# Layer two's output product by seven products for half of two column blocks, the spatial masks delayed, and the last block's copies rearranged

## The chip, the cores and the metric

The kernel runs on one core of a Trainium2 chip. The metric is device time in microseconds (us), the median of three runs. TensorE multiplies, VectorE (DVE) and ScalarE (ACT) do elementwise work, GpSimd (POOL) a little of it, and SyncE (SP) starts most of the transfers. Each engine executes its own instructions in the order in which the program issues them, and waits where an instruction's input or its buffer isn't ready.

## The reference

Two layers over 256 tokens of width 2048, all in fp32:

```python
def reference(x, ...):
    for l in range(DEPTH):                                   # 2
        h = rms_norm(x, norm1_g[l])
        z = h @ w_in[l]                                      # [sgu u | sgu v | q | k | v]
        z_sgu = jax.nn.gelu(z[..., :2 * SGU_WIDTH], approximate=False)
        out_a = chunked_sgu(z_sgu, sgu_norm_g[l], sgu_w[l], sgu_b[l])
        out_b = swa_sink_attention(...)                      # 16 heads, 4 groups, window 128
        mixed = jnp.concatenate([rms_norm(out_a, out_norm_a[l]),
                                 rms_norm(out_b, out_norm_b[l])], axis=-1)
        x = x + mixed @ w_out[l]                             # 2048 x 2048
        h2 = rms_norm(x, norm2_g[l])
        x = x + (jax.nn.silu(h2 @ w_gate[l]) * (h2 @ w_up[l])) @ w_down[l]
    return x

def chunked_sgu(z, v_norm_g, w_s, b_s):
    u, v = jnp.split(z, 2, axis=-1)
    v = rms_norm(v.reshape(...), v_norm_g)                   # 16 heads, chunks of 128
    w = w_s * jnp.tril(jnp.ones((CHUNK, CHUNK), w_s.dtype))
    gate = jnp.einsum('hts,bcshd->bcthd', w, v) + b_s.T[None, None, :, :, None]
    return u * gate.reshape(b, s, SGU_WIDTH)
```

The feed-forward width is 5632.

## The kernel before

**The unit of work.** TensorE takes an fp32 product as three products of rounded operands (type fp32r): `mm3` (lines 149 to 151) multiplies high part by high, high part by the weight's low part, and low part by the weight's high part. A weight tile of 256 x 512 is loaded by `raw_load` on SP (line 106, 512 KB, eight buffers). `split2` casts it to its high part `wh` on ACT (line 115, five buffers) and forms the low part `wl` on DVE (line 116, four buffers). A `unit` multiplies one such tile with both token halves: 2 x 2 x 3 = 12 matmuls of 128x512 into two PSUM banks.

**Order.** The program is issued in one stream, and each engine keeps that order. A unit advances a clock by one (`tick`), a half unit by 0.5; side work (norms, transposes, attention) is put into the stream by `later(delay, fn)` when the clock gets there. PSUM has eight banks: five for products (`acc`), two beside (`dacc`), one small (`sm`). Small products (transposes, attention, spatial gate) take their bank in turn from `sm`, `dacc`, `dacc`, `acc`.

**Normalising.** `inv_rms` writes mean square plus epsilon `ms` on DVE (line 203) and takes its power of -1/2 on POOL (`ir`, line 205). POOL's queue also holds the bias loads (line 516) and, per half of the spatial gate, the load of `wm` (line 607) with the triangular mask directly behind it (`affine_select`, line 608). Line 639 scales `v` by `ir` on DVE.

**The output product.** `mixed @ w_out` has four column blocks of 512 (0 to 3) and two halves: `a` (spatial gate, four pairs of 128 rows) and `b` (attention, likewise). A part such as a1 is half `a` of column block 1: four units, each of one pair, into two banks. When a part is whole, DVE adds it to the residual `xres`, scaled by that half's inverse rms (line 757, one instruction per token half). When both parts of a block are whole, `norm_block` takes the block's transposes for the second norm. The table `PARTS` sets the order in which the units of the parts are issued, one row per layer. The pairs are made from transposes (`ps_t`, line 222) by `split_gain`: ACT writes the high part with the gain (line 212), DVE the low part (line 213), into `aT`.

**Seven products.** Feed-forward blocks and part of the q projection use `seven`, a scheme with seven products of half-size operands instead of eight (2 x 2 blocks of the token halves against the even and odd tiles of k, by two column blocks). It needs sums of the operands: sums of weight tiles (on DVE, line 332, or by transfers that add, on POOL) and sums of activation tiles, formed by `combine`: `g` on ACT (line 266), `e` in three DVE instructions (lines 274 and 277 are the first two), the split into `ext` on ACT and DVE (line 287). Its products lie in five banks.

**The end.** The last product, `w_down`, adds into banks that were seeded with the residual. `out_of` copies a finished bank to SBUF on ACT (line 889) and stores it from SP (line 891); in the last column block each token half goes in two quarters.

Of the kernel before, what the change touches and what calls it, by code (L numbers as in the profile page):

```python
# [12 lines left out]
F32 = mybir.dt.float32  # L13
# [7 lines left out]
P = 128  # L21
# [42 lines left out]
END_AT = (((22, 26), (30, 32)), ((22, 27), (31, 33)))  # L64
FF_FIRST = 5
EXT_AT = (6.5, 8, 11, 13, 16, 18, 21.5, 24)
GATE_LOAD = ((24, 29), (5, 15))
PARTS = (
    "a0 a0 a1 a1 a0 a0 a1 a1 a2 a2 a2 a2 a3 a3 a3 a3 b0 b0 b1 b1 b0 b0 b1 b1 b2 b2 b2 b2 b3 b3 b3 b3",
    "a0 a0 a1 a1 a0 a0 a1 a1 b0 b0 b0 b0 b1 b1 b1 b1 a2 a2 a2 a2 b2 b2 b2 b2 a3 a3 a3 a3 b3 b3 b3 b3",  # L70
# [14 lines left out]
def trunk(ctx, tc, x, xt, w_in, w_q, w_out, w_gate, w_up, w_down, sgu_w, sgu_g, consts,  # L85
# [206 lines left out]
    def combine(ps, lay, col, ext):  # L292
# [4 lines left out]
        extend(g, ap, "big", ext)  # L297
        return pair

    def seven(src, pairs, ext, out, end=lambda sg: None, soon=False, by_dma=(), put_off=False):  # L300
# [79 lines left out]
        yield  # L380

# [41 lines left out]
    for lay in range(L):  # L423
# [180 lines left out]
        def gate_load(b, lay=lay, wms=wms):  # L604
            wm = ap.tile([P, 8, P], F32, tag="big", name="wm", bufs=8)
            with tc.issue_after(anchor[0].ins):
                nc.gpsimd.dma_start(wm, sgu_w[lay, :, 8 * b : 8 * b + 8, :])
            nc.gpsimd.affine_select(
                out=wm, in_=wm, pattern=[[0, 8], [1, P]], compare_op=ALU.is_ge, fill=0.0,
                base=0, channel_multiplier=-1,  # L610
            )
            wms[b] = wm

# [39 lines left out]
        pairs_a = []  # L653

        def u_gated(b, acc, lay=lay, layer=layer, gate=gate, ssa=ssa, pairs_a=pairs_a):
# [79 lines left out]
        def finish_mixed(kind, ss, rstds=rstds):  # L735
            rstds[kind] = finish_rms(ss, SW)

# [140 lines left out]
        def down(blocks, lay=lay, pairs_f=pairs_f, norm_block=norm_block, ss1=ss1, pairs1=pairs1, ext1=ext1, left=left, live=live, release=release, accs=accs, full=full, seed=seed, flush=flush, turn_over=turn_over):  # L878
# [4 lines left out]
            def out_of(n, t, acc):  # L883
                parts = 2 if last and n == ND - 1 else 1
                w = NB // parts
                for i in range(parts):
                    cs = slice(n * NB + i * w, n * NB + (i + 1) * w)
                    xs = xres[:, t, cs]
                    nc.scalar.copy(xs, acc[:, i * w : (i + 1) * w])
# [160 lines left out]
```

## Time and profile before

| what | us |
|---|---|
| three runs | 1920.44 to 1922.36, median 1920.5 |
| the profiled execution | 1919.74 |
| its span | 1918.0 |
| TensorE busy, 0 to 200 us | 195.81 |
| TensorE busy, 1000 to 1146.6 us | 146.58 |
| TensorE busy, 1146.6 to 1212 us | 65.40 |
| TensorE busy, 1212 to 1400 us | 188.00 |
| TensorE busy, 1800 to 1918 us | 113.50 |
| DVE busy in the same five stretches | 159.66, 105.88, 46.25, 172.99, 82.76 |

The span is the time from the first to the last event of the profiled execution. The granted TensorE clock is 1.00 throughout, and the core moves 453.71 MB at a mean of 237 GB/s. In a group of the profile, `x` is followed by the count, then by busy time and mean ns of one, and then by the idle time of the engine just before these instructions and the releaser that ended most of it. In a timeline, a row is start, duration, engine, line, operation, output<-inputs, and in brackets the wait before it and what ended it. In a table by window, the columns are the sum, then the busy time of PE, PEld, DVE, ACT and POOL (count in parentheses), then granted clock, DMA share and GB/s.

### The profile page before, as it was taken

The page shows a single profiled execution, that of the slowest core. Times are in us where ns is not written, and L with a number is a line of the kernel's source. Part 1 is how long each engine was busy: PE and PEld are TensorE (multiplying, and loading weights), DVE is VectorE, ACT ScalarE, POOL GpSimd, SP SyncE. Part 2 cuts the span into 40 slices and gives each one's busy share as a digit, 9 for nine tenths or more (in the row PEclk, how much of TensorE's full clock was granted, in tenths as well). Part 3 has the DMA queues.
Part 4 walks back from the last instruction along what each step waited for, and adds up shares of the span by engine and source line. Part 5 has one row for each costly group of instructions (what it writes and reads, how often), then busy time and mean ns, then how long its engine had stood idle before and what let it go on. Part 6 is the DMA issues. An engine that isn't in the chain of part 4 may idle for free.

```text
span 1918.0 us, 25387 instructions
## 1 busy us (share of the span) xinstructions
PE 1909.3 (100%) x8788; PEld 1571.2 (82%) x8788; DVE 1693.5 (88%) x1826; ACT 1343.2 (70%) x1799; POOL 170.0 (9%) x172
## 2 busy tenths in 40 slices
PE   9999999999999999999999999999999999999999
PEld 7878888888888888888888888888888888888887
DVE  7986689999999999999796767799999999999993
ACT  8668576677667676777777576566877677766774
POOL 0221001000100001000011200000000100010000
PEclk9999999999999999999999999999999999999999
DMA  9874348788877897888577534587789778888783
GB/s 354 260 272 159 136 160 238 257 243 283 262 238 248 270 290 228 247 256 287 187 220 258 188 126 164 179 265 234 246 264 295 231 248 260 282 239 254 252 274 110
DMA packets 126707, 453.71 MB, mean 237 GB/s; under 512 B 14065, under 2 KB 14705, under 8 KB 126577
## 3 DMA queue, kind: packets, MB, share of 16 engines
q1 hardware_dynamic: 105264, 375.52, 53.0%
q0 software_dynamic: 20736, 75.51, 21.2%
q8 instruction: 69, 1.13, 0.2%
q10 hardware_dynamic: 576, 1.05, 0.2%
q14 instruction: 62, 0.50, 0.1%
HBM read 449.92 MB, written 2.10 MB: 236 GB/s over the span
## 4 chain that ended last, share of the span: by engine, by line
PE 94%; issue 1%; DVE 1%; DMA 1%; POOL 1%; ACT 0%; SPq 0%; ACTq 0%; DVEq 0%; POOLq 0%
PE m L150 14%; PE m L149 14%; PE m L151 14%; PE dacc L149 10%; PE dacc L150 10%; PE dacc L151 10%; PE acc L149 6%; PE acc L151 5%; PE acc L150 5%; PE ps_f L222 1%; PE ps_v L578 1%; DMA wm<-in_sgu_w_dram 1%; DVE wl L116 1%; PE ps_s L529 1%; POOL ir L205 1%
## 5 line engine op out<-in xcount | busy, mean ns | idle before, releaser
L115 ACT CAST wh<-raw 128x1024 fp32r<-128x1024 f32 (+1 forms) x794 | 815.9, 1050 | 417.6 <-DVE raw L332 166.9
L116 DVE TENSOR_TENSOR wl<-raw,wh 128x1024 fp32r<-128x1024 f32 (+1 forms) x794 | 945.3, 1219 | 106.0 <-PE acc L150 29.3
L149 PE MATMUL m<-wh,ext 128*128 128x512 f32 x704 | 276.7, 393 | 0.0
L150 PE MATMUL m<-wl,ext 128*128 128x512 f32 x704 | 274.9, 390 | 0.0
L151 PE MATMUL m<-wh,ext 128*128 128x512 f32 x704 | 274.4, 390 | 0.0
L150 PE MATMUL dacc<-wl,aT 128*128 128x512 f32 x624 | 243.3, 390 | 0.0
L149 PE MATMUL dacc<-wh,aT 128*128 128x512 f32 x624 | 243.2, 391 | 0.0
L151 PE MATMUL dacc<-wh,aT 128*128 128x512 f32 x624 | 243.0, 389 | 0.0
L116 DVE TENSOR_TENSOR wl<-t,wh 128x1024 fp32r<-128x1024 f32 x176 | 213.3, 1222 | 12.7 <-issue 5.2
L115 ACT CAST wh<-t 128x1024 fp32r<-128x1024 f32 x176 | 184.4, 1051 | 38.0 <-DVE t L333 14.1
L150 PE MATMUL m<-wl,hT 128*128 128x512 f32 x528 | 205.8, 390 | 1.7 <-DVE wl L116 1.7
L149 PE MATMUL m<-wh,hT 128*128 128x512 f32 x528 | 206.4, 391 | 0.0
L151 PE MATMUL m<-wh,hT 128*128 128x512 f32 x528 | 205.6, 389 | 0.0
L150 PEld LDWEIGHTS m<-wl,ext 128*128 128x128 f32 x704 | 132.2, 188 | 28.7 <-DVE wl L116 1.8
L149 PEld LDWEIGHTS m<-wh,ext 128*128 128x128 f32 x704 | 132.2, 188 | 27.6 <-ACT wh L115 0.9
L151 PEld LDWEIGHTS m<-wh,ext 128*128 128x128 f32 x704 | 132.1, 188 | 27.5
L149 PEld LDWEIGHTS dacc<-wh,aT 128*128 128x128 f32 x624 | 117.1, 188 | 25.2 <-ACT wh L115 0.8
L150 PEld LDWEIGHTS dacc<-wl,aT 128*128 128x128 f32 x624 | 117.2, 188 | 24.7 <-DVE wl L116 0.6
L151 PEld LDWEIGHTS dacc<-wh,aT 128*128 128x128 f32 x624 | 117.1, 188 | 24.4
L149 PE MATMUL acc<-wh,aT 128*128 128x512 f32 x336 | 135.0, 402 | 0.0
L151 PE MATMUL acc<-wh,aT 128*128 128x512 f32 x336 | 131.5, 391 | 0.0
L150 PE MATMUL acc<-wl,aT 128*128 128x512 f32 x336 | 130.9, 390 | 0.0
(151 smaller groups left out, 2717.0 us busy)
## 6 DMA issues: line engine op xcount, KB each, us to landing
raw<-in_w_gate_dram SPq DMA_DIRECT2D x176, 512.0 KB, 5.8
raw<-in_w_up_dram SPq DMA_DIRECT2D x176, 512.0 KB, 5.7
raw<-in_w_down_dram SPq DMA_DIRECT2D x176, 512.0 KB, 5.7
t<-in_w_gate_dram POOLq DMA_DIRECT2D x80, 512.0 KB, 7.4
raw<-in_w_in_dram SPq DMA_DIRECT2D x76, 512.0 KB, 5.7
raw<-in_w_out_dram SPq DMA_DIRECT2D x64, 512.0 KB, 3.2
raw<-in_w_up_dram POOLq DMA_DIRECT2D x40, 512.0 KB, 6.0
raw<-in_w_q_dram SPq DMA_DIRECT2D x32, 512.0 KB, 5.2
```

What stands on the lines that cost most here:

```text
L115: nc.scalar.copy(wh[:, j : j + step, :], src)
L116: nc.vector.tensor_tensor(wl[:, j : j + step, :], src, f(wh[:, j : j + step, :]), ALU.subtract)
L149: nc.tensor.matmul(acc, ah, wh, start=first, stop=False, skip_group_check=again)
L150: nc.tensor.matmul(acc, ah, wl, start=False, stop=False, skip_group_check=again)
L151: nc.tensor.matmul(acc, al, wh, start=False, stop=last, skip_group_check=again)
L205: anchor[0] = nc.gpsimd.tensor_tensor(r, ms, mhalf[:, :n], ALU.pow)
L222: nc.tensor.transpose(ps[:, j, t * P : (t + 1) * P], blocks[t][:, j * P : (j + 1) * P], ident)
L529: nc.tensor.matmul(ps[r][:, i, :], qT[gp][rows, i0 + i, t * P : (t + 1) * P], kT[rows, gp, :nk], start=True, stop=True,)
L578: nc.tensor.matmul(pv[:, r, i], pt[:, (r * n + i) * (t + 1) + b, :], zkv[b][:, cols], start=b == 0, stop=b == t,)
```

## The change

Three edits go together.

**Layer two's output product.** Half `a` of column blocks 2 and 3, which was two parts of four units, becomes fourteen steps "s" of `seven_low`: seven products of two halves each, a half being six matmuls. It uses three banks, `l0`, `l1` and `l2`, in place of `seven`'s five. The weights come from a new host array `w_oa`, the same values in another order. Per two pairs, the tiles x and b22 take raw buffers, `ys` and `ss` take buffers of the tag "hT"; DVE adds two sums (lines 433 and 434), POOL issues two adding transfers (lines 435 and 440). ACT copies bank l0 into l1 once and two partial results into `mp`; DVE adds to these, and adds the four results to the residual (`residual`, at one step each, two with the negated inverse rms `na`). The pairs of half `a` are now made by `combine_a`, which also makes the sums `ext`. While steps "s" are open, small products take their bank from three places and not four. The table's second row sets where the steps stand among the units of a0, a1, b0 and b1.

**Masks.** The triangular mask is issued 5 (layer two: 4) clock units after its load and behind the last power or transfer that POOL has been given by then.

**Last copies.** In the last column block only the second token half goes in two quarters; the second quarter is copied by DVE, and the first quarter's store is issued by ACT's queue.

```diff
--- before.py
+++ after.py
+S_OUT = (False, True)
+EXT_A_WAIT = 0.5
+MASK_AFTER = ((5, 5), (4, 4))
...
-    "a0 a0 a1 a1 a0 a0 a1 a1 b0 b0 b0 b0 b1 b1 b1 b1 a2 a2 a2 a2 b2 b2 b2 b2 a3 a3 a3 a3 b3 b3 b3 b3",
+    "a0 a0 s a0 s a0 a1 a1 s a1 s a1 s b0 s b0 s b0 s b0 s b1 s b1 s b1 s b1 s s b2 b2 b2 b2 b3 b3 b3 b3",
...
     solo = [False]
+    few = [False]
...
-        pool, tag = ((pm, "sm"), (pd, "dacc"), (pd, "dacc"), (pa, "acc"))[next(turns) % 4]
+        homes = ((pm, "sm"), (pd, "dacc"), (pd, "dacc"), (pa, "acc"))
+        pool, tag = homes[next(turns) % (3 if few[0] else 4)]
         return pool.tile(shape, F32, tag=tag, name=name)
...
-    def extend(g, pool, tag, ext, wait=1):
+    def extend(g, pool, tag, ext, wait=1, e=None):
-        e = zp.tile([P, 4, P], F32, tag="z", name="e")
+        e = zp.tile([P, 4, P], F32, tag="z", name="e") if e is None else e
...
+    def combine_a(ps, lay, col, ext):
+        ge = tp.tile([P, 2, NB], F32, tag="hT", name="ge")
+        g = ge[:, 0].rearrange("p (j c) -> p j c", j=2)
+        for j in range(2):
+            nc.scalar.activation(
+                g[:, j, :], ps[:, j, :], AF.Copy, scale=cst[:, lay, col + j : col + j + 1]
+            )
+        pair = tp.tile([P, 2, 2, SEQ], F32R, tag="aT", name="aT")
+        nc.scalar.copy(pair[:, 0], g)
+        nc.vector.tensor_tensor(pair[:, 1], g, f(pair[:, 0]), ALU.subtract)
+        extend(g, tp, "hT", ext, EXT_A_WAIT, ge[:, 1].rearrange("p (n c) -> p n c", n=4))
         return pair
...
         yield
+    def seven_low(src, pairs, ext, out):
+        def half(raw, acc, op, i, first=False, stop=False):
+            wh, wl = split2(raw)
+            for j in range(2):
+                ah, al = (op(2 * i + j, h) for h in range(2))
+                mm3(
+                    acc, ah, al, wh[:, j, :], wl[:, j, :], first and i + j == 0,
+                    stop and i + j == 2, not first,
+                )
+            tick(0.5)
+        def a_op(k, t):
+            return lambda p, h: pairs[p][:, h, k, t * P : (t + 1) * P]
+        def e_op(n):
+            return lambda p, h: ext[p][:, h, n, :]
+        def bank(name):
+            return pa.tile([P, NB], F32, tag="acc", name=name)
+        def held(name):
+            return tp.tile([P, 2, NB], F32, tag="hT", name=name)
+        x, y, s = [], [], []
+        acc0 = bank("l0")
+        for i in range(2):
+            x.append(raw_load(src(0, 0, i)))
+            y.append(held("ys"))
+            nc.sync.dma_start(y[i], src(0, 1, i))
+            b22 = raw_load(src(1, 1, i))
+            s.append(held("ss"))
+            half(x[i], acc0, a_op(0, 0), i, True, True)
+            yield
+            nc.vector.tensor_tensor(x[i], x[i], y[i], ALU.add)
+            nc.vector.tensor_tensor(s[i], x[i], b22, ALU.add)
+            anchor[0] = nc.gpsimd.dma_start(y[i], src(1, 1, i), accum_op=ALU.add)
+        acc1 = bank("l1")
+        nc.scalar.copy(acc1, acc0)
+        for i in range(2):
+            half(s[i], acc1, e_op(2), i, False, True)
+            anchor[0] = nc.gpsimd.dma_start(s[i], src(1, 0, i), accum_op=ALU.add)
+            yield
+        mp = wp.tile([P, 2, NB], F32, tag="raw", name="mp", bufs=8)
+        nc.scalar.copy(mp[:, 0], acc1)
+        acc2 = bank("l2")
+        for i in range(2):
+            half(y[i], acc2, e_op(0), i, True, True)
+            yield
+        nc.scalar.copy(mp[:, 1], acc2)
+        for i in range(2):
+            half(raw_load(src(1, 0, i)), acc0, a_op(1, 0), i, False, True)
+            yield
+        out(0, 0, acc0, 1)
+        for i in range(2):
+            half(x[i], acc1, e_op(1), i, False, True)
+            yield
+        nc.vector.tensor_tensor(mp[:, 1], acc1, mp[:, 1], ALU.add)
+        for i in range(2):
+            half(s[i], acc2, a_op(1, 1), i, False, True)
+            yield
+            if i == 0:
+                out(1, 1, mp[:, 1], -1)
+        nc.vector.tensor_tensor(mp[:, 0], acc2, mp[:, 0], ALU.add)
+        for i in range(2):
+            half(raw_load(src(1, 1, i)), acc1, e_op(3), i, False, True)
+            yield
+            if i == 0:
+                out(0, 1, mp[:, 0], 1)
+        out(1, 0, acc1, -1)
...
                 nc.gpsimd.dma_start(wm, sgu_w[lay, :, 8 * b : 8 * b + 8, :])
-            nc.gpsimd.affine_select(
-                out=wm, in_=wm, pattern=[[0, 8], [1, P]], compare_op=ALU.is_ge, fill=0.0,
-                base=0, channel_multiplier=-1,
-            )
             wms[b] = wm
+            def mask():
+                with tc.issue_after(anchor[0].ins):
+                    nc.gpsimd.affine_select(
+                        out=wm, in_=wm, pattern=[[0, 8], [1, P]], compare_op=ALU.is_ge, fill=0.0,
+                        base=0, channel_multiplier=-1,
+                    )
+            later(MASK_AFTER[lay][b], mask)
...
+        ext_a = []
...
                 ps = transpose_pair([us[t][:, 2 * c * P : (2 * c + 2) * P] for t in range(NTOK)])
-                pairs_a.append(split_gain(ps, lay, C_GA + 4 * b + 2 * c, "aT"))
+                if S_OUT[lay]:
+                    pairs_a.append(combine_a(ps, lay, C_GA + 4 * b + 2 * c, ext_a))
+                else:
+                    pairs_a.append(split_gain(ps, lay, C_GA + 4 * b + 2 * c, "aT"))
...
-        def finish_mixed(kind, ss, rstds=rstds):
+        def finish_mixed(kind, ss, lay=lay, rstds=rstds):
+            if kind == "a" and S_OUT[lay]:
+                na = small([P, NTOK], "na")
+                def negate():
+                    for t in range(NTOK):
+                        nc.vector.tensor_scalar(
+                            na[:, t : t + 1], rstds["a"][t], -1.0, None, ALU.mult
+                        )
+                later(3, negate)
+                rstds["na"] = [na[:, t : t + 1] for t in range(NTOK)]
...
+        def residual(n, t, c, sign, rstds=rstds):
+            xs = xres[:, t, n * NB : (n + 1) * NB]
+            r = rstds["a"][t] if sign > 0 else rstds["na"][t]
+            nc.vector.scalar_tensor_tensor(xs, c, r, xs, ALU.mult, ALU.add)
         parts = {}
+        whole = {}
+        def complete(n, whole=whole, ss2=ss2, pairs2=pairs2, ext2=ext2, norm_block=norm_block):
+            whole[n] = whole.get(n, 0) + 1
+            if whole[n] == 2:
+                norm_block(n, ss2, pairs2, lay, C_G2, ext2)
+        low = seven_low(
+            lambda r, c, i: w_oa[lay, c, i, r], pairs_a, ext_a,
+            lambda c, t, acc, sign: residual(2 + c, t, acc, sign),
+        )
+        n_low = 0
         for name in PARTS[lay].split():
+            if name == "s":
+                few[0] = True
+                next(low)
+                n_low += 1
+                continue
...
                 parts[name] = [part(kind, n), 0]
+            if n_low == 14:
+                next(low, None)
+                few[0] = False
+                n_low += 1
+                for m in range(2, ND):
+                    complete(m)
             next(parts[name][0])
...
                 next(parts[name][0], None)
-                if all(parts.get(f"{k}{n}", (0, 0))[1] == NKV for k in "ab"):
-                    norm_block(n, ss2, pairs2, lay, C_G2, ext2)
+                complete(n)
         rstd2 = finish_rms(ss2, D)
...
             def out_of(n, t, acc):
-                parts = 2 if last and n == ND - 1 else 1
+                parts = 2 if last and n == ND - 1 and t == NTOK - 1 else 1
                 w = NB // parts
...
                     xs = xres[:, t, cs]
-                    nc.scalar.copy(xs, acc[:, i * w : (i + 1) * w])
+                    by_vector = i == 1 and t == 1
+                    (nc.vector.tensor_copy if by_vector else nc.scalar.copy)(
+                        xs, acc[:, i * w : (i + 1) * w]
+                    )
                     if last:
-                        nc.sync.dma_start(out[t * P : (t + 1) * P, cs], xs)
+                        queue = nc.scalar if parts > 1 and t == 1 and i == 0 else nc.sync
+                        queue.dma_start(out[t * P : (t + 1) * P, cs], xs)
                 if t == NTOK - 1 and final and lay < L - 1:
...
+        "w_oa": _parities(a["w_out"][:, :SW, 2 * NB :]),
```

How the instructions move is shown at three places, in each engine's order of issue.

On POOL in layer one, before the change, where an `ir` with 16 columns is a power of `v` or q, and one with 8 that of k:

```order
L608 AFFINE_SELECT wm<-wm 128x1024
L607 DMA wm<-in_sgu_w_dram 128x1024
L516 DMA bias<-in_band_dram 128x1024 x2
L608 AFFINE_SELECT wm<-wm 128x1024
L205 TENSOR_TENSOR ir_1099<-ms_1097,mhalf 128x16
L205 TENSOR_TENSOR ir_1182<-ms_1180,mhalf 128x8
L205 TENSOR_TENSOR ir_1273<-ms_1271,mhalf 128x16
```

With the change:

```order
L700 AFFINE_SELECT wm<-wm 128x1024
L695 DMA wm<-in_sgu_w_dram 128x1024
L604 DMA bias<-in_band_dram 128x1024 x2
L210 TENSOR_TENSOR ir_1098<-ms_1096,mhalf 128x16
L210 TENSOR_TENSOR ir_1181<-ms_1179,mhalf 128x8
L700 AFFINE_SELECT wm<-wm 128x1024
L210 TENSOR_TENSOR ir_1273<-ms_1271,mhalf 128x16
```

The second mask has moved behind two powers.

On TensorE at the start of part a1 in layer two, before the change (acc_10155 is a bank of part a0, acc_10243 and acc_10244 are those of a1, `ps_t` the transposes for the pairs of half `a`):

```order
L151 MATMUL acc_10155<-wh,aT 128x512
L578 MATMUL ps_v<-zkv,pt 128x64 x8
L222 MATMUL ps_t<-ident,u 128x128 x4
L149 MATMUL acc_10243<-wh,aT 128x512
L150 MATMUL acc_10243<-wl,aT 128x512
L151 MATMUL acc_10243<-wh,aT 128x512
L149 MATMUL acc_10244<-wh,aT 128x512
```

With the change (l_10261 is bank l0, acc_10387 and acc_10388 are those of a1):

```order
L156 MATMUL l_10261<-wh,aT 128x512
L227 MATMUL ps_t<-ident,ob 128x128 x4
L227 MATMUL ps_t<-ident,u 128x128 x4
L154 MATMUL acc_10387<-wh,aT 128x512
L155 MATMUL acc_10387<-wl,aT 128x512
L156 MATMUL acc_10387<-wh,aT 128x512
L154 MATMUL acc_10388<-wh,aT 128x512
L155 MATMUL acc_10388<-wl,aT 128x512
L156 MATMUL acc_10388<-wh,aT 128x512
L154 MATMUL acc_10387<-wh,aT 128x512
L654 MATMUL ps_p<-ident,s 128x128 x2
L155 MATMUL acc_10387<-wl,aT 128x512
```

A half product of `l0` and eight transposes now stand directly ahead of a1's first unit, and the third unit of a0 has moved behind it.

On DVE at the same place, before the change, from the split that TensorE needs for a1 on (`ob` and `rden` are attention's, `tot` and `ms` the norm of half `a`):

```order
L116 TENSOR_TENSOR wl<-raw,wh 128x1024
L585 TENSOR_TENSOR ob<-ps_v,rden 128x2x128
L233 TENSOR_REDUCE tot<-ssa 128x2
L203 TENSOR_SCALAR ms_10285<-tot 128x2
L213 SCALAR_TENSOR_TENSOR aT<-ps_t,cst,aT 128x256 x2
L571 TENSOR_TENSOR rden<-den,es 128x4
L572 RECIPROCAL rden<-rden 128x4
L213 SCALAR_TENSOR_TENSOR aT<-ps_t,cst,aT 128x256 x2
L116 TENSOR_TENSOR wl<-raw,wh 128x1024
```

With the change (`ge` holds a pair with its sums, `na` is the negated inverse rms, `ys` a weight sum):

```order
L633 TENSOR_TENSOR es<-nm,nsink 128x4
L238 TENSOR_REDUCE tot<-ssa 128x2
L119 TENSOR_TENSOR wl<-raw,wh 128x1024
L279 TENSOR_TENSOR ge<-ge 128x256
L208 TENSOR_SCALAR ms_10326<-tot 128x2
L282 SCALAR_TENSOR_TENSOR ge<-ge 128x128
L839 TENSOR_SCALAR na<-ir_10328 128x1 x2
L285 SCALAR_TENSOR_TENSOR ge<-ge 128x128
L314 TENSOR_TENSOR aT<-ge,aT 128x512
L433 TENSOR_TENSOR raw<-raw,ys 128x1024
```

Between the split and the low part of the pair now stand the sums of the pair and, between `ms` and the pair, the negation `na`, whose input comes from POOL.

On DVE around the end of part a1 in layer two, before the change:

```order
L116 TENSOR_TENSOR wl<-raw,wh 128x1024
L213 SCALAR_TENSOR_TENSOR aT<-ps_t,cst,aT 128x256 x2
L757 SCALAR_TENSOR_TENSOR xres<-acc_10243,ir_10287,xres 128x512
L757 SCALAR_TENSOR_TENSOR xres<-acc_10244,ir_10287,xres 128x512
L116 TENSOR_TENSOR wl<-raw,wh 128x1024 x2
L213 SCALAR_TENSOR_TENSOR aT<-ps_t,cst,aT 128x256 x2
L116 TENSOR_TENSOR wl<-raw,wh 128x1024 x2
```

With the change:

```order
L119 TENSOR_TENSOR wl<-raw,wh 128x1024
L119 TENSOR_TENSOR wl<-ys,wh 128x1024
L218 SCALAR_TENSOR_TENSOR aT<-ps_t,cst,aT 128x256 x2
L865 SCALAR_TENSOR_TENSOR xres<-acc_10387,ir_10328,xres 128x512
L865 SCALAR_TENSOR_TENSOR xres<-acc_10388,ir_10328,xres 128x512
L119 TENSOR_TENSOR wl<-raw,wh 128x1024
L119 TENSOR_TENSOR wl<-ys,wh 128x1024
L119 TENSOR_TENSOR wl<-raw,wh 128x1024 x8
```

The splits around a1's residual sums are now those of half products (from `ys` and `raw`) in turn with b0's units.

More of the change, by code (lines that the diff above doesn't have):

```diff
@@ L84, in trunk @@
 @with_exitstack
-def trunk(ctx, tc, x, xt, w_in, w_q, w_out, w_gate, w_up, w_down, sgu_w, sgu_g, consts,
+def trunk(ctx, tc, x, xt, w_in, w_q, w_out, w_oa, w_gate, w_up, w_down, sgu_w, sgu_g, consts,
           band, out):
@@ L297, in combine @@
         extend(g, ap, "big", ext)
+        return pair
+    def combine_a(ps, lay, col, ext):
[9 more added lines that the diff above has]
+        extend(g, tp, "hT", ext, EXT_A_WAIT, ge[:, 1].rearrange("p (n c) -> p n c", n=4))
         return pair
@@ L653, in trunk, with u_gated @@
         pairs_a = []
-        def u_gated(b, acc, lay=lay, layer=layer, gate=gate, ssa=ssa, pairs_a=pairs_a):
+        ext_a = []
+        def u_gated(b, acc, lay=lay, layer=layer, gate=gate, ssa=ssa, pairs_a=pairs_a, ext_a=ext_a):
             us = []
```

## The prediction

> **What bounds the kernel now.** I read the page's first rows, then the waits of TensorE, then stretches by window, then the timeline at the places that the change touches.
>
> ```profile
> PE 1909.3 (100%) x8788; PEld 1571.2 (82%) x8788; DVE 1693.5 (88%) x1826; ACT 1343.2 (70%) x1799; POOL 170.0 (9%) x172
> PE m L150 <- DVE wl L116: 1.7, 1, 1.7
> PE heat L188 <- DVE mhalf L190: 1.5, 1, 1.5
> PE acc L149 <- ACT wh L115: 0.7, 1, 0.7
> ```
>
> TensorE is busy for 1909.3 of 1918.0 us. Its longest wait after the start is a single one of 1.7 us, on a split (`wl`). So only three things change the time: fewer matmuls, a wait taken away or added on TensorE, and what lies behind the last matmul.
>
> ```profile
> 1893.62 0.39 PE L149 MATMUL acc<-wh,aT 128*128 128x512 f32 x1
> 1896.34 0.39 PE L149 MATMUL acc<-wh,aT 128*128 128x512 f32 x1
> ```
>
> Twelve matmuls lie between these starts (one unit): 2.72 us, so **0.227 us a matmul**; the 0.39 shown is its whole passage, 0.17 of it beside the next one.
>
> **Term 1: fewer matmuls.** The `a` half of two column blocks is now 2 x 4 units of 12 = 96 matmuls. Seven products of two halves with six matmuls each are 84. Twelve are removed: 12 x 0.227 = **-2.72 us**. Transposes and attention products stay as many.
>
> **Term 2: the mask in layer one.** The 1.7 us wait has its origin on POOL:
>
> ```profile
> 106.59 0.17 DVE L203 TENSOR_SCALAR ms<-hs 128x16 f32<-128x16 f32 x1
> 105.22 1.07 POOL L516 DMA_DIRECT2D bias<-in_band_dram  x2
> 111.81 1.09 POOL L608 TENSOR_SCALAR_AFFINE_SELECT wm<-wm 128x1024 f32<-128x1024 f32 x1 [5.52 <-DMA wm<-in_sgu_w_dram]
> 112.87 2.93 POOL L205 TENSOR_TENSOR ir<-ms,mhalf 128x16 f32<-128x16 f32 x1
> 110.40 0.42 DVE L247 TENSOR_REDUCE hs<-sq 128x4 f32<-128x256 f32 x1
> 115.83 0.69 DVE L639 TENSOR_TENSOR v<-v,ir 128x512 f32<-128x512 f32 x1 [5.01 <-POOL ir L205]
> 117.11 2.36 DVE L116 TENSOR_TENSOR wl<-t,wh 128x1024 fp32r<-128x1024 f32 x2
> 116.34 0.39 PE L149 MATMUL m<-wh,hT 128*128 128x512 f32 x1
> 118.39 0.50 PE L150 MATMUL m<-wl,hT 128*128 128x512 f32 x1 [1.67 <-DVE wl L116]
> ```
>
> The power's input `ms` is there at 106.76, but the power stands on POOL behind a mask that waits for its load until 111.81. DVE then stands for 5.01 us at `v<-v,ir`, with the split that TensorE needs queued behind it. In the new order two powers come ahead of that mask. The first can start at 106.9 and ends by 109.8 at 2.93 us, or by 110.8 at the slowest such power (3.894, quoted below), before DVE's queue comes to `v` at 110.82. The DVE stall goes, and 5 us of lead cover the 2.05 between the two TensorE starts: 2.05 - 0.23 = **-1.82 us**. The mask itself moves to about 114, behind the second power; its reader, the second spatial product, comes a block later. Bounds: 0 (the next split is late instead) and -1.9.
>
> **Term 3: the end.**
>
> ```profile
> 1913.11 0.39 PE L151 MATMUL acc<-wh,aT 128*128 128x512 f32 x1
> 1912.86 1.38 ACT L889 COPY xres<-acc 128x256 f32<-128x256 f32 x4 [9.61 <-PE acc L151]
> 1913.25 2.16 SPq L891 DMA_DIRECT2D out_dram<-xres  x4
> 1914.43 0.99 SPq L891 DMA_DIRECT2D out_dram<-xres  x2
> out_dram<-xres SPq DMA_DIRECT2D x4, 128.0 KB, 2.0
> ```
>
> Matmuls end at 1913.50, four copies at 1914.24, but four issues on SP only at 1915.41; the last starts about 1914.9 and lands 2 us later. Now the first token half is one copy and one issue, the last two quarters are copied by ACT and DVE side by side (about 0.35 each) and issued from two queues at about 1914.0 to 1914.15. The last issue starts **0.75 us** earlier. Bounds 0.3 (ACT's issue lands half a microsecond later) and 1.1 (the whole time by which the issues trail the copies).
>
> **Term 4: new waits in layer two.** This is the uncertain one.
>
> ```profile
> 1146.61:1175.00 28.39, 28.39 (x148) 23.90 (x146) 18.40 (x30) 17.19 (x32) 1.41 (x2) 1.00 0.43 149
> L116 DVE TENSOR_TENSOR wl<-raw,wh 128x1024 fp32r<-128x1024 f32 x32 | 38.9, 1222 | 13.1 <-PE acc L150 9.6 <-ACT void L229 1.3 <-issue 1.2
> L757 DVE SCALAR_TENSOR_TENSOR xres<-acc,ir,xres 128x512 f32<-128x512 f32 x15 | 10.6, 746 | 4.1 <-PE acc L151 4.1
> L213 DVE SCALAR_TENSOR_TENSOR aT<-ps_t,cst,aT 128x256 fp32r<-128x256 f32 x10 | 4.7, 483 | 4.1 <-ACT aT L212 4.1
> L287 DVE TENSOR_TENSOR ext<-e,ext 128x512 fp32r<-128x512 f32 x6 | 4.1, 683 | 0.0
> L274 DVE TENSOR_TENSOR e<-g 128x256 f32<-128x256 f32 x6 | 2.6, 426 | 3.9 <-ACT g L266 3.9
> L277 DVE SCALAR_TENSOR_TENSOR e<-e,g 128x128 f32<-128x128 f32 x6 | 1.8, 292 | 0.2
> L332 DVE TENSOR_TENSOR raw<-raw x88: 1217/1225/1227, 29.0 to 1836.0; 128x1024 f32<-128x1024 f32 x88
> L205 POOL TENSOR_TENSOR ir<-ms,mhalf x18: 692/2734/3894, 43.8 to 1238.9; 128x2 f32<-128x2 f32 x8, 128x16 f32<-128x16 f32 x8, 128x8 f32<-128x8 f32 x2
> 1147.29 0.71 POOL L205 TENSOR_TENSOR ir<-ms,mhalf 128x2 f32<-128x2 f32 x1 [49.00 <-DVE ms L203]
> t<-in_w_gate_dram POOLq DMA_DIRECT2D x80, 512.0 KB, 7.4
> ```
>
> Before, DVE has 18.40 us of work in 28.39 us of TensorE there, and its splits run ahead until TensorE gives a buffer back (9.6 us of idle on `acc L150`). The change adds on DVE: six more splits (14 halves against 8 units) 6 x 1.22 = 7.3; four weight sums by the 1.22 of L332, 4.9; for each of four pairs 2.4 (0.69 + 0.43 + 2 x 0.29 + 0.69) in place of two of 0.48, 5.8 in all; two partial sums 1.4: **19 us**, most of it in this stretch. From the split of a1's first unit to that of the second half of product three stand 39 DVE instructions, 28.1 us by these rows. Rows that follow each other start about 0.08 sooner than they end (106.59 + 0.17 against the next at 106.67), so they need about 25, against about 29 us that TensorE needs from there. DVE is not the bound, but it loses its lead, and its queue is in order. Counting forward from 1146.61, where the two TensorE orders part, I find TensorE waiting at these places:
>
> ```profile
> 1146.61 0.47 PE L149 MATMUL acc<-wh,aT 128*128 128x512 f32 x1
> 1149.46 0.60 PE L222 MATMUL ps_t<-ident,ob 128*128 128x128 f32 x4
> 1149.89 0.60 PE L222 MATMUL ps_t<-ident,u 128*128 128x128 f32 x4
> ```
>
> (a) a1's first unit is now placed ahead of a0's third. Of four `wl` buffers three hold splits not yet read, so its split starts when the first half has been read: 1146.61 + 6 x 0.227 + 0.17 = 1148.14, and ends at 1149.4. TensorE has eight transposes (0.43 per four) and one matmul with the high part first, until 1149.1: wait 0.3.
> (b) Behind that split on DVE stand 0.43 + 0.17, the power on POOL (0.15 to start, 0.71), two negations of 0.15 that wait for it, 0.29 and the low part of pair three, 0.69: done at 1152.1. TensorE, from 1149.45, has six matmuls, two transposes (0.2), another matmul and two with the high part: 1151.7. Wait 0.4.
> (c) a1 ends at t. Its two banks go to b0, so b0's second matmul waits for two residual sums (0.75 each), which start at t + 0.2 and end at t + 1.6; TensorE is there at t + 1.36 + 0.23: wait 0.1. Behind the sums on DVE stands b0's split, done at t + 2.75; TensorE gets there at t + 1.9: wait 0.8. The bank wait comes once more at b1: 0.1.
>
> Sum **+1.7 us**. The other places come out with 0.3 to 3 us to spare. Bounds: 0 (the lead holds) and 4.8 (rows at full length without the overlap, 3.1 more). The transfers cost nothing: two accumulating loads for `ys` leave POOL at about 1153 and are read at about 1170, the loads of that size that POOL issues landing after a median of 7.4; the stretch's DMA share is 0.43, and 10 transfers of SP and 4 of POOL take the place of 8. If that cover goes, ACT's casts come late microsecond by microsecond.
>
> **Sum.** -2.72 - 1.82 - 0.75 + 1.7 = -3.6 us. The profiled run took 1919.74 us (span 1918.0 and 1.74 around it), so 1916.1 by it; it lies 0.8 below the median of 1920.5, and by the median **1916.9 us**.
>
> **Rivals.**
> 1. *The lead holds, no new wait*: -5.3, **1915.2 us**. For: 9.6 us of DVE idle against buffers. Against: waits (a) and (c) follow from buffers and queue order, not from load.
> 2. *The mask's stall moves to the next late split*: term 2 is 0, **1918.7 us**. For: splits around 118 to 122 have little lead. Against: DVE gains 5 us there.
> 3. *The power of (b) takes 3.9 us and not 0.71.* DVE stands at the negation as long: +3.2, **1920.1 us**. For: the row of powers spans 692 to 3894 ns. Against: behind `ms` DVE has a single short operation before it waits, and with DVE mostly idle the same 128x2 power took 0.71. The Trainium skill ("SBUF — State Buffer", "Who interferes with whom") says that a DVE instruction with two SBUF inputs and a GpSimd instruction that reads SBUF shut each other out, each for its whole length. The spread of the row agrees with that, and by the rule the power waits here for one operation of 0.29 only.
> 4. *DVE becomes the bound of the 28 us* (slower): 28.1 us at full length, and the ACT-fed operations leave the idle that the rows show, 4.1/10 per `aT` (six of them) and 3.9/6 per `e` (two), 3.8 us. Waits then are 1.7 + 3.1 + 3.8 = 8.6, and the time **1923.8 us**. It decides once the waits pass 5.3. Against: before, DVE had nothing else due in those idle times; now splits stand there.
>
> That the change doesn't do what it says is out for the matmuls, which are counted in the program.
>
> **How the numbers follow.** Chances: forecast 0.53, rival 1 0.17, rival 2 0.09, rival 3 0.07, rival 4 0.10, the rest 0.04. The forecast's own range is 1915.9 to 1918.2. The range of 1915.2 to 1919.8 takes in both bounds of term 4 and rivals 1 and 2; rivals 3 and 4 lie outside. A change under 0.2% (3.8 us) can't be told from none here, so the line for faster is 1916.7: rival 1 and four tenths of the forecast lie below it, with a little of the rest 0.40. Slower by over 0.2% needs 1924.3, about half of rival 4 with a little of the rest: 0.06. Within: 0.54.
>
> **What would show it.** TensorE's matmul count 12 lower; no wait of TensorE on `wl` near 118, and DVE's 5.0 us on POOL's `ir` gone; the last output issue about 0.5 us, not 1.4, behind the last matmul; in layer two TensorE waits on `wl` and `aT` of 0.3 to 0.8 us at a1's first unit, a0's third and b0's first. A wait above 1.5 us on DVE or ACT between 1146 and 1212, or waits that sum to 4 us or more, would make it wrong; so would a TensorE wait on a load there.

## The result, and the profile after

The changed kernel takes **1916.56 us**, the median of 11 runs (1915.77 to 1918.4); before it is 1920.5 us (1920.21 to 1924.78, 11 runs beside them). The ratio is 0.9977, with a 95% interval of 0.9969 to 0.9985: faster by 0.15 to 0.31%. The profiled execution took 1915.77 us, its span is 1914.0 (1918.0 before).

The first part of the page and the longest waits of TensorE, as they stand after the change (lines 149 to 151 are now 154 to 156, the splits 118 and 119):

```profile
PE 1907.2 (100%) x8776; PEld 1569.2 (82%) x8776; DVE 1709.5 (89%) x1853; ACT 1353.1 (71%) x1814; POOL 182.5 (10%) x176
PE heat L193 <- DVE mhalf L195: 1.5, 1, 1.5
PE acc L154 <- ACT wh L118: 0.9, 1, 0.9
```

TensorE has 12 instructions fewer, and its wait of 1.7 us on a split is gone. What is left stands at the start of the program.

**The mask.** Rows of the timeline around the place where TensorE stood (start, duration, then the instruction; in brackets the wait before it):

```profile
107.07 3.83 POOL L210 TENSOR_TENSOR ir<-ms,mhalf 128x16 f32<-128x16 f32 x1 [0.56 <-DVE ms L208]
111.82 6.63 POOL L210 TENSOR_TENSOR ir<-ms,mhalf 128x8 f32<-128x8 f32 x1 [0.92 <-DVE ms L208]
118.41 2.36 POOL L700 TENSOR_SCALAR_AFFINE_SELECT wm<-wm 128x1024 f32<-128x1024 f32 x1
110.99 0.67 DVE L732 TENSOR_TENSOR v<-v,ir 128x512 f32<-128x512 f32 x1
116.55 0.39 PE L154 MATMUL m<-wh,hT 128*128 128x512 f32 x1
116.78 0.39 PE L155 MATMUL m<-wl,hT 128*128 128x512 f32 x1
```

The power starts at 107.07, ahead of the mask, and ends at 110.90, just before DVE comes to `v` at 110.99: no wait is left there, and the two TensorE starts lie 0.23 apart instead of 2.05.

**Layer two's output product.** TensorE, DVE and POOL at a1's first unit and up to the low part of the next pair:

```profile
1146.38 1.22 DVE L119 TENSOR_TENSOR wl<-raw,wh 128x1024 fp32r<-128x1024 f32 x1 [0.86 <-PE l L155]
1147.20 0.47 PE L154 MATMUL acc<-wh,aT 128*128 128x512 f32 x1
1147.66 0.19 PEld L155 LDWEIGHTS acc<-wl,aT 128*128 128x128 f32 x1 [0.29 <-DVE wl L119]
1148.17 0.72 POOL L210 TENSOR_TENSOR ir<-ms,mhalf 128x2 f32<-128x2 f32 x1 [51.54 <-DVE ms L208]
1148.92 0.21 DVE L839 TENSOR_SCALAR na<-ir 128x1 f32<-128x1 f32 x2 [0.65 <-POOL ir L210]
1149.25 0.69 DVE L314 TENSOR_TENSOR aT<-ge,aT 128x512 fp32r<-128x512 f32 x1
1150.07 0.39 PE L154 MATMUL acc<-wh,aT 128*128 128x512 f32 x1
1150.30 0.40 PE L156 MATMUL acc<-wh,aT 128*128 128x512 f32 x1
```

The split ends at 1147.60 and TensorE reads it at 1147.66, 0.46 behind its last start: a wait of 0.23 (the next step, 0.33, is longer too: 0.34 over the two). DVE stands 0.65 us for POOL's power, yet the low part is written at 1149.94, and the matmul that reads it starts at 1150.30, 0.23 behind the one before it: no wait.

The same engines where a1 ends and b0 begins:

```profile
1170.79 0.39 PE L156 MATMUL acc<-wh,aT 128*128 128x512 f32 x1
1171.22 1.43 DVE L865 SCALAR_TENSOR_TENSOR xres<-acc,ir,xres 128x512 f32<-128x512 f32 x2
1171.47 0.39 PE L156 MATMUL acc<-wh,aT 128*128 128x512 f32 x1
1172.57 1.22 DVE L119 TENSOR_TENSOR wl<-raw,wh 128x1024 fp32r<-128x1024 f32 x1
1173.51 0.39 PE L154 MATMUL l<-wh,ext 128*128 128x512 f32 x1
1173.84 0.19 PEld L155 LDWEIGHTS acc<-wl,aT 128*128 128x128 f32 x1 [0.36 <-DVE wl L119]
1174.17 0.40 PE L156 MATMUL acc<-wh,aT 128*128 128x512 f32 x1
```

b0's split ends at 1173.79 and TensorE reads it at 1173.84: its starts are 0.33 and 0.33 apart, so 0.2 us over two normal steps. The two places together are 0.54 us. No other wait of this size is left in the stretch.

**The end.** The last copies and stores, with TensorE's last matmul:

```profile
1909.18 1.11 ACT L1025 COPY xres<-acc 128x512 f32<-128x512 f32 x2 [9.61 <-PE acc L156]
1909.43 0.39 PE L156 MATMUL acc<-wh,aT 128*128 128x512 f32 x1
1909.79 1.31 SPq L1030 DMA_DIRECT2D out_dram<-xres  x2
1910.31 0.35 ACTq L1030 DMA_DIRECT2D out_dram<-xres  x1
1910.32 0.42 DVE L1025 COPY xres<-acc 128x256 f32<-128x256 f32 x1 [10.28 <-ACT xres L1025]
```

Matmuls end at 1909.82. DVE's copy does not run beside ACT's: ACT's ends at 1910.29, DVE's begins at 1910.32. SP's last store is issued at 1910.77, 0.95 us behind the last matmul, where it was 1.39.

**Where the 4 us came from**, in TensorE's start times against the profile of before (a minus is earlier; 120.5 is just behind the old wait, 1112.5 lies before layer two's output product, 1241.3 behind it):

| profiled execution | 16.7 us | 115.0 | 120.5 | 1112.5 | 1241.3 | end of the last matmul |
|---|---|---|---|---|---|---|
| the change | -0.05 | +0.21 | -1.77 | -1.66 | -3.88 | -3.68 |

The mask is the step from +0.21 to -1.77, **-1.98**. The seven products are the step from -1.66 to -3.88, **-2.22**. The stores are the rest of the span, 3.93 - 3.68 = **0.25**, of which the last landing behind the last matmul (3.48 before, 3.29 now) is 0.2. The three make 4.45; 0.5 of it was lost again at other places (+0.21 by 115.0, +0.11 from 120.5 to 1112.5, +0.20 behind 1241.3).

### The profile page after: what moved, and what is told of

Same layout as the page of the kernel before. It is cut to its first block, busy times and chain, and to the rows that moved or that the text cites. A ratio compares the mean times of both kernels' runs of the same rounds, so it can differ in the third digit from the quotient of the medians.

```text
span 1914.0 us, 25417 instructions
## 1 busy us (share of the span) xinstructions
PE 1907.2 (100%) x8776; PEld 1569.2 (82%) x8776; DVE 1709.5 (89%) x1853; ACT 1353.1 (71%) x1814; POOL 182.5 (10%) x176
## 3 DMA queue, kind: packets, MB, share of 16 engines
q8 instruction: 68, 1.11, 0.2%
q10 hardware_dynamic: 720, 1.18, 0.2%
## 4 chain that ended last, share of the span: by engine, by line
PE 97%; issue 1%; DVE 1%; ACT 0%; POOL 0%; DMA 0%; SPq 0%; DVEq 0%; ACTq 0%; POOLq 0%
PE m L155 15%; PE m L154 15%; PE m L156 15%; PE dacc L154 11%; PE dacc L155 11%; PE dacc L156 11%; PE acc L154 5%; PE acc L155 5%; PE acc L156 5%; PE ps_v L666 1%; PE ps_f L227 1%; PE ps_s L617 1%; PE ps_n L227 1%; PE ps_p L654 0%; PE ps_t L227 0%
## 5 line engine op out<-in xcount | busy, mean ns | idle before, releaser
L154 PE MATMUL acc<-wh,aT 128*128 128x512 f32 x304 | 121.8, 402 | 0.0
L359 POOL DMA_DIRECT2D t<-in_w_gate_dram x80 | 69.3, 866 | 524.7 <-DVE wl L119 393.1
L156 PE MATMUL acc<-wh,aT 128*128 128x512 f32 x304 | 119.1, 392 | 0.0
```

What stands on the lines that cost most here:

```text
L154: nc.tensor.matmul(acc, ah, wh, start=first, stop=False, skip_group_check=again)
L156: nc.tensor.matmul(acc, al, wh, start=False, stop=last, skip_group_check=again)
L359: anchor[0] = nc.gpsimd.dma_start(t2, src(1, 0, i), accum_op=ALU.add)
```

## The experiments

Each kernel was timed in turn with the kernel before: 11 runs of each, against 15 to 33 of the kernel before, whose median was 1920.44 to 1920.78 in these series. The times scatter by 2 to 5 us within one kernel, and the table at the end of this section shows where the profiled executions differ; so the text goes by TensorE's start times wherever a step is smaller than that. The expectations were written with the trace above known, so where they repeat its numbers the run tests only whether the edit alone brings them.

**The seven products alone** (the masks and the last copies as before):

```diff
-            later(MASK_AFTER[lay][b], mask)
+            nc.gpsimd.affine_select(out=wm, in_=wm, ...)
...
-                parts = 2 if last and n == ND - 1 and t == NTOK - 1 else 1
+                parts = 2 if last and n == ND - 1 else 1
```

> The seven products alone, masks and last copies as before. Theory: 12 matmuls fewer (-2.7 us) less some 0.5 us of new waits of TensorE, so 2.2 us below before, about 1918.3; between the end of layer two's attention and the feed-forward TensorE waits only about 0.2 us each at a1's first unit and at b0's first. Rival (the waits as predicted, 1.7 us): 1.0 us below before, about 1919.5. Rival (no wait at all): 2.7 us below, 1917.8. The wait of 1.7 us near 118 us stays.

Measured: 1920.42 us, ratio 0.9995 (0.9986 to 1.0004). The median alone can't be told from no change, and misses the expected 1918.3 by 2.1 us; six of the 11 runs took 1920.4 or more, and what those lost no trace shows. The profiled execution took 1918.6. In it the product's stretch is 2.19 us shorter, as in the change (2.22), and the wait near 118 us is still there:

```profile
PE m L155 <- DVE wl L119: 1.6, 1, 1.6
```

So the theory holds for the stretch, and neither rival does.

**The masks alone:**

```diff
-            nc.gpsimd.affine_select(out=wm, in_=wm, ...)
+            later(MASK_AFTER[lay][b], mask)
```

> The mask behind the powers, alone. Theory: TensorE's wait near 118 us goes and no split after it is late: 1.8 us below before, about 1918.7, and TensorE reaches 289 us of before at about 287.2. Rival (the next split is late instead): no gain, 1920.5.

Measured: 1918.69 us, ratio 0.9988 (0.9979 to 0.9997). TensorE gains 1.98 us at that place and keeps it to the end. The rival, in which the next split is late instead, is out. The place expected for 289 us of before missed its number, since this execution was already 0.72 us behind at 115 us.

**The last copies alone:**

```diff
-                parts = 2 if last and n == ND - 1 else 1
+                parts = 2 if last and n == ND - 1 and t == NTOK - 1 else 1
...
+                    (nc.vector.tensor_copy if by_vector else nc.scalar.copy)(
...
+                        queue = nc.scalar if parts > 1 and t == 1 and i == 0 else nc.sync
```

> The last copies alone. Theory: DVE's copy starts only when ACT's quarter has been copied, so the last store is issued about 0.95 us behind the last matmul and not 1.39: 0.3 to 0.45 us below before, about 1920.1. Rival (as predicted, side by side): issue at 0.5 to 0.65 us, 0.75 us below, 1919.75.

Measured: 1920.67 us, ratio 0.9999 (0.9991 to 1.0008), which tells neither the theory nor the rival from no change. The rows of its end:

```profile
1915.30 1.11 ACT L890 COPY xres<-acc 128x512 f32<-128x512 f32 x2 [9.61 <-PE acc L151]
1915.92 1.31 SPq L895 DMA_DIRECT2D out_dram<-xres  x2
1916.44 0.35 ACTq L895 DMA_DIRECT2D out_dram<-xres  x1
1916.44 0.42 DVE L890 COPY xres<-acc 128x256 f32<-128x256 f32 x1 [10.28 <-ACT xres L890]
```

DVE waits for ACT here too, and the last store is issued 0.95 us behind the last matmul. It lands at 3.31. With the old copies three profiles have 3.48, 3.50 and 3.60, with the new ones six have 3.24 to 3.89, the middle of them 3.3. So the issue comes 0.44 earlier each time, and the landing some 0.2 by the medians, with a scatter that is larger. From its issue the last store took 2.09 to 2.21 us in the three old profiles and 2.29 to 2.94 in the six new ones; why it takes longer wasn't shown.

The Trainium skill ("PSUM — Partial Sum Buffer", section "PSUM bank collisions raise a hardware error") says that ScalarE and VectorE may not access one PSUM bank on the same partitions at the same time, two reads included, and that software has to keep them apart. The trace agrees as far as it can: both quarters lie in one bank, and DVE's copy waits for ACT's in each of these kernels. Copying them side by side from one bank was not tried for that reason. The profile names the tile `xres` as what DVE waits for, and both copies write it too; but that tile alone does not hold two engines apart. After the change DVE writes a part of it while ACT reads another:

```profile
1206.66 0.74 DVE L872 SCALAR_TENSOR_TENSOR xres<-mp,ir,xres 128x512 f32<-128x512 f32 x1
1206.71 0.63 ACT L234 ACTIVATE void<-xres 128x512 bf16<-128x512 f32 x1
```

So the bank is the likely cause. Two quarters in two banks, which would show it, were not tried.

**The second token half in one piece:**

```diff
-                parts = 2 if last and n == ND - 1 and t == NTOK - 1 else 1
+                parts = 1
...
-                    by_vector = i == 1 and t == 1
+                    by_vector = False
```

> The changed kernel with the second token half of the last block copied whole by ACT and stored by one issue from SP. Theory: the copy takes 0.59 us, the issue starts about 0.73 us behind the last matmul (0.95 in the change), and the store of twice the size lands as much later as the issue is earlier: within 0.3 us of the change, about 1916.6. Rival (the wait of DVE's copy is the whole loss, size costs nothing): 0.2 us below the change.

Measured: 1916.67 us, ratio 0.9978 (0.9969 to 0.9987), the same as the change. The last store is issued 0.72 us behind the last matmul and takes 2.94 us to land, where the quarter took 2.34: the landing is at 3.66, not 3.29. In this one profile the larger store costs more than the shorter chain of copies gains; but the six profiles with quarters land at 3.24 to 3.89 and their store takes up to 2.94 us as well, so an effect of the size isn't shown.

**The negation later:**

```diff
-                later(3, negate)
+                later(6, negate)
```

> The changed kernel with the two negations three clock units later. The prediction's place (b) put 0.4 us of TensorE's waiting on DVE standing there for POOL's power. Theory now: DVE stands 0.65 us, but the low part of the pair comes in time, so nothing is gained: 1916.6, within 0.2. If (b) was right: 0.4 below, 1916.2, and the wait of TensorE ahead of the low part goes.

Measured: 1917.04 us, ratio 0.9981 (0.9972 to 0.999). But the edit did not move the negations. DVE has all its operations in the same order as in the change, and stands just as long:

```profile
1150.69 0.21 DVE L839 TENSOR_SCALAR na<-ir 128x1 f32<-128x1 f32 x2 [0.65 <-POOL ir L210]
1150.82 0.28 DVE L285 SCALAR_TENSOR_TENSOR ge<-ge 128x128 f32<-128x128 f32 x1
```

So this run says nothing about the negation; it is the change once more. Its stretch repeats (2.20 us shorter than before, 2.22 in the change), and its median lies 0.5 us above the first one. That the negation costs nothing rests on the change's own trace, where the low part is there before the matmul that reads it.

**More work for DVE in the stretch.** Two extra weight sums for each of the two pairs, each a repeat of the sum before it:

```diff
             nc.vector.tensor_tensor(s[i], x[i], b22, ALU.add)
+            for _ in range(2):
+                nc.vector.tensor_tensor(s[i], x[i], b22, ALU.add)
```

> The changed kernel with four more weight sums on DVE, each a repeat of the second sum of its pair (the result is the same). They are 4 x 1.22 us, about 4.6 with the overlap, all ahead of the splits of product l1 that TensorE reads 1.07 and 1.09 us after they end. Theory (DVE is not the bound, but has only about one microsecond of lead there): TensorE waits 3.5 to 4 us in that place, 1920.1 to 1920.6, less what a1's later waits then spare. Rival 1 of the prediction (9.6 us of idle absorb it): no change, 1916.6. Rival 4 (DVE is the bound already): the full 4.6 to 4.9, 1921.3.

Measured: 1922.46 us, ratio 1.001 (1.0001 to 1.0019), more than the theory or either rival gave. The stretch is 5.2 us longer than in the change, which rules out rival 1. From its timeline, and then from its table by window:

```profile
1168.31 0.50 PE L155 MATMUL l<-wl,ext 128*128 128x512 f32 x1 [2.31 <-DVE wl L119]
1170.52 0.79 PE L154 MATMUL l<-wh,ext 128*128 128x512 f32 x1 [0.78 <-ACT wh L118]
1171.54 0.63 PE L156 MATMUL acc<-wh,aT 128*128 128x512 f32 x1
1171.97 0.63 PE L155 MATMUL acc<-wl,aT 128*128 128x512 f32 x1
```

```profile
1165.00:1170.50 5.50, 2.43 (x10) 1.36 (x8) 5.50 (x7) 1.08 (x2) 1.33 (x2) 0.95 0.79 152
1170.50:1174.00 3.50, 3.48 (x10) 2.76 (x11) 3.50 (x8) 2.24 (x3) 1.89 (x2) 0.59 0.95 213
```

DVE is busy for all of 9.0 us. The two waits make TensorE's starts 2.47 and 0.95 us later, 3.4 in all, which is what the theory gave (4.6 less 1.07). The expectation missed the rest, 1.8 us. Most of it, about 1.4, is the granted clock. The 0.59 above is a mean; in narrower windows the clock is halved for 3.4 us:

```profile
1166.00:1169.90 3.90, 1.43 (x5) 0.86 (x5) 3.90 (x4) 0.48 (x1) 0.86 (x1) 1.00 0.86 139
1169.90:1173.30 3.40, 2.78 (x7) 2.20 (x8) 3.40 (x7) 2.84 (x4) 1.28 (x2) 0.50 0.89 175
1173.30:1174.00 0.70, 0.70 (x5) 0.56 (x4) 0.70 (x3) 0.00 (x0) 0.61 (x1) 0.97 0.96 263
```

Meanwhile one matmul's step is 0.59 us and five are 0.43, instead of 0.227. The other 0.4 lies in short waits.

**Half of that:** one extra sum per pair.

> The changed kernel with two more weight sums on DVE (one per pair), about 2.3 us ahead of product l1's splits, where four of them cost 5.3 us of TensorE's time by the trace: 3.4 of waits there and the rest at a granted clock of 0.59 behind them. Theory: the lead of about 1.07 us is used up first, 1.2 to 1.4 us of waits are left, and a wait of that size doesn't lower the clock: 1.2 to 1.6 us more than the change by the trace, about 1918. Rival (the cost is in proportion): half of 5.3, 1919.2. Rival (no slack, DVE the bound): 2.3 or more.

Measured: 1919.22 us, ratio 0.9993 (0.9984 to 1.0002). The stretch is 1.78 us longer than in the change. Its one long wait, and the clock behind it:

```profile
PE l L154 <- ACT wh L118: 1.5, 1, 1.5
1165.00:1170.50 5.50, 4.00 (x20) 3.14 (x19) 5.48 (x10) 3.75 (x6) 1.68 (x2) 1.00 1.00 215
```

The clock stays at 1.00. So 2.3 us of DVE work cost 1.8 and 4.6 cost 5.2: a slack of half a microsecond to one, then the full price, then the clock on top. The median alone would speak for the rival in proportion, whose 1919.2 it meets. In the trace the stretch costs less than that rival's 2.6 and the other's 2.3, a little more than the theory's 1.2 to 1.6, and 0.7 us (0.2 in the change) were lost behind the stretch, where the kernels don't differ; so the theory has the better of it, on one profile. The added sums also move a few neighbours in the order of DVE and TensorE, so the slack is known to some tenths only.

**Seven products in layer one too:**

```diff
-S_OUT = (False, True)
+S_OUT = (True, True)
...
-    "a0 a0 a1 a1 a0 a0 a1 a1 a2 a2 a2 a2 a3 a3 a3 a3 b0 b0 b1 b1 b0 b0 b1 b1 b2 b2 b2 b2 b3 b3 b3 b3",
+    "a0 a0 s a1 a1 s a0 s a0 s a1 s a1 s s s s s s s s s b0 b0 b1 b1 b0 b0 b1 b1 b2 b2 b2 b2 b3 b3 b3 b3",
```

> The changed kernel with seven products in layer one's output product as well, its steps between a0 and a1 and behind them, since the attention half is ready only some 20 units later. Twelve matmuls fewer: if no new wait comes, 2.7 us below the change, 1913.9. If the splits of fourteen halves in a row are the bound (1.22 us each against six matmuls of 1.36, beside layer one's attention and the sums), TensorE waits several us there and the time is 1916.6 or more. I expect about 1916.

Measured: 1917.9 us, ratio 0.9988 (0.9979 to 0.9997). Twelve matmuls fewer should have made layer one 2.7 us shorter; from 120.5 to layer two's first spatial product TensorE needs 1.54 us more than before, so 4.3 us went into waits, none of them long. The largest piece, 2.1 us by the sum of their start-to-start times, is attention's transposes. Timeline of ACT and TensorE:

```profile
195.97 0.40 ACT L638 ACTIVATE s<-s,nm 128x128 f32<-128x128 f32 x1 [2.89 <-DVE nm L632]
196.52 3.03 PE L654 MATMUL ps_p<-ident,s 128*128 128x128 f32 x8
196.90 0.14 PEld L654 LDWEIGHTS ps_p<-ident,s 128*128 128x128 f32 x1 [0.25 <-ACT s L638]
197.29 0.14 PEld L654 LDWEIGHTS ps_p<-ident,s 128*128 128x128 f32 x1 [0.25 <-ACT s L638]
```

ACT's exponentials wait 2.89 us for DVE, which is late, and TensorE, which had come to their transposes, then takes them at ACT's pace of 0.39 each: eight in 3.0 us. In the 11 us ahead of that place (185 to 196) DVE is busy for 9.7, so it has little room there for the half products' splits and sums; which of them made it late was not followed further. This version doesn't beat the change, and takes 2 us more than the expected 1916.

TensorE's start times against the profile of before, for all of them (us):

| profiled execution | 16.7 us | 115.0 | 120.5 | 1112.5 | 1241.3 | mask step | product step |
|---|---|---|---|---|---|---|---|
| the change | -0.05 | +0.21 | -1.77 | -1.66 | -3.88 | -1.98 | -2.22 |
| seven products alone | +0.33 | +0.43 | +0.32 | +0.33 | -1.86 | -0.11 | -2.19 |
| masks alone | +0.50 | +0.72 | -1.26 | -1.24 | -1.24 | -1.98 | 0.00 |
| last copies alone | +1.18 | +2.54 | +2.50 | +2.50 | +2.50 | -0.04 | 0.00 |
| second half in one piece | +0.68 | +0.87 | -1.11 | -0.67 | -2.89 | -1.98 | -2.22 |
| negation later (not moved) | +1.06 | +1.74 | -0.24 | +0.11 | -2.09 | -1.98 | -2.20 |
| four more sums | +0.65 | +1.78 | -0.20 | -0.24 | +2.77 | -1.98 | +3.01 |
| seven products in both layers | +0.21 | +0.52 | -1.45 | +0.36 | -1.80 | -1.97 | -2.16 |
| two more sums | +0.15 | +0.53 | -1.44 | -1.31 | -1.75 | -1.97 | -0.44 |

The first two columns show the scatter: up to 1.2 us are lost in the first 16.7 us, and up to 2.5 by 115, in one profiled execution and not in the next, whatever the kernel; what decides it was not looked for. The last two columns repeat within 0.06 us for kernels that share an edit, the product step of the two with added sums aside.

## Why the prediction was right

It put the time at 1916.9 us, 3.6 below before, and 1916.56 was measured, inside its own range. Terms 1 and 2 were right in mechanism and size. Term 4 was right about two of its three places and too large, and term 3 had a step wrong. These two errors, 1.2 us too slow and 0.5 too fast, cancel in part, and the medians show 0.5 us less gain than the terms of the profile; so that the forecast lies only 0.3 us from the median is in part luck.

- **Term 1, fewer matmuls (-2.72): right.** The count is 12 lower, and the product step is -2.22 with 0.54 of longer steps in it, which makes -2.76.
- **Term 2, the mask (-1.82): right**, at -1.98. The order of events was as told, though with less margin: the power took 3.83 us, near the slow end that the prediction allowed (110.8; it was 110.90), and DVE came 0.09 us later. The mask went to 118.4, not 114, behind a power that took 6.63, and its reader did not wait for it. Rival 2 is out in all seven kernels with the edit.
- **Term 3, the end (-0.75): about 0.2 to 0.3.** The step that failed is "copied by ACT and DVE side by side". They go one after the other (most likely because both read one bank, which was not tested by itself), so the last issue is 0.95 us behind the last matmul and not 0.5 to 0.65. Of the 0.44 us by which it is earlier, part goes to a landing that takes longer (2.34 us; 2.09 before). The stated lower bound, 0.3, was nearer.
- **Term 4, new waits (+1.7): about 0.5.** Two of three places were right, and the sum was too large. (a) was forecast at 0.3 and is 0.34 over its two steps. (b), 0.4, is nothing, for two reasons of like size. The chain on DVE from the split to the low part was summed with rows at full length (2.7 us), although the prediction itself had noted that rows that follow each other overlap by 0.08; it took 2.34. And TensorE needs 2.64 us (1147.66 to 1150.30) to come to the low part and not 2.25: its order has one matmul more there than was counted, and some longer steps. (c), 1.0 with the bank waits, is 0.2: the sums were made to start when a1 ends, but a1's first bank is finished three matmuls before its second (TensorE rows at 1170.79 and 1171.47), so DVE starts at 1171.22, and everything behind it on DVE is 0.7 us earlier.
- **Rival 1 (no new wait), 1915.2:** nearly so in this stretch, where 0.5 of the 1.7 us came. Its reason, that DVE has 9.6 us of idle to spare, fell: two more sums already cost 1.8 us.
- **Rival 3 (the power of (b) takes 3.9):** out. It took 0.72, with one DVE operation of 0.29 beside it.
- **Rival 4 (DVE is the bound):** out for the change, but near. With 4.6 us more on DVE the kernel is slower than before.
- **The range:** with term 4 at its upper bound of 4.8 the sum gives 1920.0, so the stated range, which ends at 1919.8, doesn't quite take that bound in. The measured time lies far from it.

By terms the profile gives -2.22 - 1.98 - 0.2 = -4.4 against -3.6 predicted. The medians give -3.9, and with the scatter of the first loads they can't tell these two apart.

## What to carry to other kernels

A new wait is priced from the instruction that really releases it: which of two banks is finished first, which rows overlap, how many instructions the waiting engine has left to do. Summing rows at full length and starting from the end of a group made the new waits more than three times too large. Two engines that share a last copy gained little here, where both read one bank; look at what each of them waits for before counting them as parallel. When a busy engine's slack is in question, give it more work in steps and read the place from the trace; the median of runs that scatter by 2 us says nothing on steps of 0.2. And look in the trace whether an edit moved what it was meant to move: the later negation stayed where it was.

## What was not expected of the hardware

TensorE's clock fell after a wait that was short. With four extra sums the granted clock fell to 0.50 at about 1169.9 and came back at about 1173.3. The wait of 2.31 us had ended 1.6 us earlier, and the next, of 0.78, had just begun; in the 3.9 us up to the fall TensorE was busy for 1.43, with five matmuls between the two waits. A single wait of 1.5 us (two extra sums) left the clock at 1.00, as the one of 1.7 us before the change had done. The Trainium skill ("TensorE: Matmul & The Clock Gate", section "Part 1: The HAM clock gate") says that the clock falls to half after an idle window of about 3.4 us. The level agrees (0.50); but here TensorE did not stand for 3.4 us at a stretch, so the clock falls after less than a whole idle window. How much idle time it takes was not tested, and it was seen in one execution only.

A power of 128x8 on POOL took 6.63 us after the change (and with the masks alone), and 2.02 before, at the same shape; the power of 128x16 ahead of it took 3.83 and 2.93. The long ones lie beside a row of DVE operations with two SBUF inputs (splits and products with `v`), while DVE's own rows keep their usual lengths there (1.21 and 0.68). So if one holds up the other in this place, it is POOL that is held up. It was not tested by itself.
